# Small score matmuls of two gated recurrences, put into the four column quarters of the matmul array

## The chip, the core and the metric

The kernel runs on one core of a Trainium2 chip. The core has a matmul engine (TensorE, PE in the profile, with its weight loads listed apart as PEld), three engines for elementwise work (VectorE or DVE, ScalarE or ACT, GpSimd or POOL), SyncE (SP) that issues DMAs, an on-chip memory of 128 partitions (SBUF), and the accumulators that TensorE writes (PSUM, 128 partitions, here eight tiles of 512 f32 columns). The metric is the device time of one execution in microseconds (us). The kernel before takes 2109.55 us, the median of three runs (2109.23 to 2110.21).

## The reference

One layer of a decoder trunk in float32: x is 256 rows of 2048. A SwiGLU half-step, a mixer, a second SwiGLU half-step, each with an RMS norm ahead and behind:

```python
h = h + 0.5 * rms_norm(swiglu(rms_norm(h, ffn1_pre), w_gate, w_up, w_down), ffn1_post)
h = h + rms_norm(mixer(rms_norm(h, mix_pre)), mix_post)
h = h + 0.5 * rms_norm(swiglu(rms_norm(h, ffn2_pre), ...), ffn2_post)
```

The mixer multiplies the row block with w_in and runs two linear recurrences, GLA (4 heads, keys of 128, values of 256) and HGRN2 (8 heads, 128 and 128). Both are the same recurrence, with a decay a between 0 and 1 for each key channel:

```python
S_t = diag(a_t) S_{t-1} + k_t v_t^T ;  o_t = S_t^T q_t
# GLA:  q = g_q / sqrt(128), a = sigmoid(code @ w_gk + b) ** (1/16)
# HGRN: q = silu(h_q), k = lc * sigmoid(-h_f), a = lb + lc * sigmoid(h_f)
merged = sigmoid(z_gla + b0) * (o_gla @ w_branch_gla) + sigmoid(z_hgrn + b1) * (o_hgrn @ w_branch_hgrn)
return merged @ w_out
```

## The kernel before, in words

**Matmuls.** The 256 rows are two tiles of 128 (t = 0, 1). Every large matmul is made of three (mm3, lines 145 to 149): the operands are split into a high and a low part in the type fp32r, and high by high, low by high and high by low are added up in PSUM. A weight chunk (two pieces of 128 by 512) is loaded by SyncE into `raw`, ScalarE writes its high part (`whi`, line 141), VectorE the rest (`wlo`, line 143), in a ring of five buffers. Some blocks are multiplied in pairs (gemm_pair, class Blocks): for chosen units of two k pieces (`sevens`) the eight products of a 2 by 2 block product are made from seven, with sums of weights on VectorE and ScalarE (`wsum`, `wsumh`, `wsuml`) and sums of the left operand that are made ahead. `FOUR` names four such units, `SUMS` three. `close` adds the shared sums to an accumulator at the end.

**Attention.** Tokens of a tile of 128 rows attend to earlier ones by levels c = 1, 2, 4, ... 64: at level c, the tile is cut into blocks of 2c tokens, and the queries of a block's right half meet the keys of its left half, each scaled with the decays between them. Behind each level VectorE multiplies kT and qT with the block totals (lines 870 and 873). A token with itself is the diagonal. `attention` (line 827) is a generator: at each `yield` it lets the large matmuls go on. It works on four heads at once, with channels in the partitions (qT, kT, 4 heads by 128 tokens in the columns):
- the diagonal (line 838): four matmuls, one for each head, of all 128 keys by all 128 queries, of which VectorE copies the diagonal into `sc` with a mask (line 840);
- levels under 32 (line 854): four matmuls, one for each head, of all 128 keys by the 64 queries in right halves, of which VectorE copies what lies in a block into `sc` with a mask (line 875);
- levels 32 and 64 (line 861): each block's left keys by its right queries; a block's result stands in the PSUM partitions of its keys, so a level-32 result takes 32 partitions, at 0 or 64. ScalarE copies it into `sc` (line 881);
- `sc` by the values, the state of tile 0 for tile 1, norm, gate, transposition (lines 890 to 934).

These matmuls are in f32, and the trace shows two weight loads and two MATMUL records for each. A matmul whose output stands in 32 of the 128 partitions uses 32 of the array's 128 columns; I call such a part a column quarter.

**What sets the order.** `Side.pump` (line 61) is called between the steps of a large matmul and lets each waiting generator go one step: those in `light` at every pump, the first two in `heavy` (the attentions, in pairs t = 0, 1) at every second one. There are three pairs: GLA, and HGRN for heads 0 to 3 and 4 to 7. On each engine the framework then orders instructions by their place in the program and by when it takes them to be ready, so neighbours on one engine can stand in another order than in the code.

**The end of a half-step.** In `down_proj` (line 567) the last seven k pieces of the second half (`tail`, line 628) are kept, and each accumulator is finished over them in turn; the left operand is split when its first matmul is written (`hkhi` on ScalarE, `hklo` on VectorE). `weigh` takes squares of the accumulator and multiplies it with the post norm's weights.

**The hgrn branch.** `two_gates` multiplies two pairs of gate blocks; behind the second pair stand four blocks of w_branch_hgrn, and `merge` (line 1126) adds each into `ms` on VectorE and transposes it for the last projection.

Of the kernel before, what the change touches and what calls it, by code (L numbers as in the profile page):

```python
# [15 lines left out]
P = 128  # L16
# [63 lines left out]
def kernel(ctx: ExitStack, tc: tile.TileContext, a: dict, out: bass.AP):  # L80
# [154 lines left out]
    class Blocks:  # L235
# [71 lines left out]
        def close(self, t, i):  # L307
            c = self.c[t][i][:, :self.w]
            add(c, c, *self.r[t, i])
# [257 lines left out]
    def down_proj(w_dram, nkt, lhs, sums_of, post, pre, wpost, ys, homes, following):  # L567
# [12 lines left out]
        def weigh(t, n):  # L580
            square(acc[t][n], ss[t], n)
            o = acc[t][n]
            if n < 2:
                o = ys()
            elif pre is None and (t, n) == (NT - 1, 3):

                o = work.tile([P, CB], F32, tag="tmp", name=nm("y"), bufs=3)

            nc.vector.tensor_tensor(o, acc[t][n], wpost[n], op=ALU.mult)
            acc[t][n] = o  # L590

        ahead = []
        for hf in range(2):
# [27 lines left out]
            if not hf:  # L621
                ahead = [split(1, kt) for kt in range(2)]
                for t in range(NT):
                    for i in range(2):
                        b.close(t, i)
                        acc[t][i] = b.c[t][i]
                        weigh(t, i)
        tail = [(kt, split(1, kt, homes[i])) for i, kt in enumerate(range(nkt - DTAIL, nkt))]
        for t in range(NT):
            for n in (2, 3):  # L630
# [6 lines left out]
                b.close(t, n - 2)  # L637
                acc[t][n] = b.c[t][n - 2]
# [119 lines left out]
    def mixer(x, rs, ready, following):  # L758
        xl = lhs_of(x)
        w_in = a["w_in"]  # L760
        with ExitStack() as mctx:
            mp = mctx.enter_context(tc.tile_pool(name="mp", bufs=1, reuse_waits="tile"))
            mp.tile([P, 56], F32, name="mfill")
# [3 lines left out]
            def blk(s, dt=F32):  # L767
                return b2.tile([P, CB], dt, tag="b", name=nm(s), bufs=30)
# [8 lines left out]
            mv = mf[:, :masked * 64].rearrange("p (l c) -> p l c", c=64)  # L777
            nc.scalar.dma_start(mv, a["c_masks"].rearrange("l p c -> p l c"))
# [9 lines left out]
            nc.scalar.dma_start(gk[16:17, :], a["gla_b_gk"])  # L788
            rq = []
# [37 lines left out]
            def attention(t, qT, kT, fT, vs, gates, dv, br, b0):  # L827
# [4 lines left out]
                sc = blk("sc")  # L832
                nc.gpsimd.memset(sc, 0.0)
                yield
                ps = ps_tile()
                for i in range(4):
                    sl = slice(i * P, (i + 1) * P)
                    nc.tensor.matmul(ps[:, sl], lhsT=kT[:, sl], rhs=qT[:, sl], start=True, stop=True)
                nc.vector.tensor_tensor(qT, qT, fT, op=ALU.mult)
                nc.vector.copy_predicated(  # L840
                    tiles4(sc), diag.unsqueeze(1).broadcast_to([P, 4, P]), tiles4(ps))
                yield
                tot, totals, at = fT, blk("tot"), 0
                for lv, c in enumerate(LEVELS):
# [5 lines left out]
                    ps = ps_tile()  # L850
                    if c < 32:
                        for i in range(4):
                            sl = slice(i * P, (i + 1) * P)
                            nc.tensor.matmul(ps[:, i * 64:(i + 1) * 64], lhsT=kT[:, sl],  # L854
                                             rhs=halves(qT[:, sl])[1], start=True, stop=True)
# [18 lines left out]
                    if c < 32:  # L874
                        nc.vector.copy_predicated(
                            halves(sc)[1],
                            masks[:, lv, :, :].rearrange("p h (b c) -> p (h b) c", c=c),
                            ps[:, :CB // 2].rearrange("p (b c) -> p b c", c=c))
                    else:
                        for r0 in range(0, P, 2 * c):  # L880
# [135 lines left out]

            def new_part(i):
# [10 lines left out]
            qT = spawn_T([scaled(q[t], rq[t], "q") for t in range(NT)], "qT")  # L1028
# [12 lines left out]
            diag = mp.tile([P, P], U8, name="diag")  # L1041
            nc.vector.tensor_copy(diag, ident)
            masks = mp.tile([P, masked, 4, 64], U8, name="masks")
# [21 lines left out]
            nc.vector.tensor_tensor(lc, lc, lm, op=ALU.mult)  # L1065

# [173 lines left out]
```

## Time and profile before

| what | value |
|---|---|
| median of the runs | 2109.55 us |
| the profiled execution, its own time | 2109.12 us |
| its span, from first to last instruction | 2107.3 us |
| mean granted TensorE clock | 0.998 |
| HBM read | 404.33 MB, 193 GB/s over the span |
| attentions (lines 838 to 861) | 864 to 1111 us of the span |

A page gives, by engine, the time that it was busy and its instructions; the views of the trace give groups of equal instructions by line, what an engine waited for and who released it, and the instructions in order of time. A group's row reads: line, engine, operation, output and inputs by the program's names, shape, count, then busy time and mean of one, then idle time before it. In a timeline row the first number is the start in us, the second the length, and a bracket gives idle time ahead of it and its releaser. [...]

### The profile page before, as it was taken

What the parts mean: (1) busy time and instruction counts of PE and PEld (TensorE: products, weight loads), DVE (VectorE), ACT (ScalarE), POOL (GpSimd) and SP (SyncE); (2) the same over time, 40 slices, a digit from 0 to 9 for tenths busy, and PEclk for the clock granted to TensorE, in tenths of its full rate; (3) what the DMA queues carried; (4) which work ended last, traced back from release to release, by engine and by line L of the source; (5) the groups of instructions that cost most, each with busy time, mean ns of one, the idle gap of its engine ahead of it and who ended that gap; (6) DMA issues with size and microseconds to landing.
All of it is one profiled execution on the core that took longest, in us unless ns stands there. A gap on an engine that the chain in (4) does not pass through costs nothing.

```text
span 2107.3 us, 27706 instructions
## 1 busy us (share of the span) xinstructions
PE 2094.5 (99%) x9874; PEld 1752.4 (83%) x9874; DVE 1796.9 (85%) x2099; ACT 1194.9 (57%) x1536; POOL 37.7 (2%) x86
## 2 busy tenths in 40 slices
PE   9999999999999999999999999999999999999998
PEld 7888888898888888888888888888888888898886
DVE  7898999999898888756577898578999999999896
ACT  6555565666565575444435555465555556566563
POOL 1000000000000100000000000010000000000000
PEclk9999999999999999999999999999999999999999
DMA  8565756656667556555555666656656666576663
GB/s 268 187 207 189 225 179 206 209 177 219 224 192 237 150 182 194 165 160 142 159 160 169 219 193 210 209 185 186 199 190 201 204 195 213 176 242 191 200 208 131
DMA packets 198012, 408.25 MB, mean 194 GB/s; under 512 B 17185, under 2 KB 25825, under 8 KB 197874
## 3 DMA queue, kind: packets, MB, share of 16 engines
q1 hardware_dynamic: 193168, 399.70, 60.4%
q10 hardware_dynamic: 4706, 6.79, 1.1%
q8 instruction: 77, 1.26, 0.2%
q14 instruction: 61, 0.50, 0.1%
HBM read 404.33 MB, written 2.10 MB: 193 GB/s over the span
## 4 chain that ended last, share of the span: by engine, by line
PE 97%; DVE 1%; DMA 1%; issue 1%; ACT 0%; POOL 0%; SPq 0%; DVEq 0%; POOLq 0%; ACTq 0%
PE c L147 19%; PE c L149 19%; PE c L148 19%; PE mm L147 6%; PE mm L149 6%; PE mm L148 6%; PE p L149 5%; PE p L148 5%; PE p L147 5%; PE ps L377 2%; PE acc L149 1%; PE acc L147 1%; PE acc L148 1%; PE ps L854 1%; DVE h L490 0%
## 5 line engine op out<-in xcount | busy, mean ns | idle before, releaser
L141 ACT ACTIVATE whi<-raw 128x1024 fp32r<-128x1024 f32 (+3 forms) x518 | 539.9, 1048 | 406.2 <-PE mm L148 180.6
L143 DVE TENSOR_TENSOR wlo<-raw,whi 128x1024 fp32r<-128x1024 f32 (+3 forms) x518 | 622.6, 1210 | 146.9 <-ACT whi L141 135.8
L147 PE MATMUL c<-whi,xhi 128*128 128x512 f32 (+1 forms) x1048 | 406.4, 388 | 0.1
L149 PE MATMUL c<-wlo,xhi 128*128 128x512 f32 (+1 forms) x1048 | 403.6, 385 | 0.0
L148 PE MATMUL c<-whi,xlo 128*128 128x512 f32 (+1 forms) x1048 | 403.5, 385 | 0.0
L233 DVE TENSOR_TENSOR wlo<-raw,whi 128x1024 fp32r<-128x1024 f32 (+1 forms) x224 | 261.5, 1202 | 8.9 <-ACT whi L268 5.2
L147 PEld LDWEIGHTS c<-whi,xhi 128*128 128x128 f32 x1048 | 196.8, 188 | 38.2 <-ACT xhi L449 0.5
L149 PEld LDWEIGHTS c<-wlo,xhi 128*128 128x128 f32 x1048 | 196.7, 188 | 38.2 <-DVE wlo L143 0.3
L148 PEld LDWEIGHTS c<-whi,xlo 128*128 128x128 f32 x1048 | 196.9, 188 | 37.0
L233 DVE TENSOR_TENSOR wsuml<-wsum,wsumh 128x1536 fp32r<-128x1536 f32 (+1 forms) x112 | 193.7, 1729 | 36.8 <-ACT wsumh L274 36.6
L148 PE MATMUL c<-whi,hklo 128*128 128x512 f32 x558 | 216.8, 389 | 1.0 <-DVE hklo L143 1.0
L147 PE MATMUL c<-whi,hkhi 128*128 128x512 f32 x558 | 217.0, 389 | 0.0
L149 PE MATMUL c<-wlo,hkhi 128*128 128x512 f32 x558 | 216.8, 388 | 0.0
L272 ACT ACTIVATE whi<-raw 128x1024 fp32r<-128x1024 f32 (+1 forms) x112 | 117.0, 1045 | 170.7 <-DVE raw L233 60.6
L147 PE MATMUL mm<-whi,xhi 128*128 128x512 f32 (+1 forms) x456 | 174.8, 383 | 0.0
L149 PE MATMUL mm<-wlo,xhi 128*128 128x512 f32 (+1 forms) x456 | 171.3, 376 | 0.0
L148 PE MATMUL mm<-whi,xlo 128*128 128x512 f32 (+1 forms) x456 | 171.0, 375 | 0.0
L270 ACT ACTIVATE wsumh<-wsum 128x1024 fp32r<-128x1024 f32 (+1 forms) x112 | 116.7, 1042 | 94.0 <-DVE wsum L233 59.4
L268 ACT ACTIVATE whi<-raw 128x1024 fp32r<-128x1024 f32 (+1 forms) x112 | 116.7, 1042 | 93.4 <-PE c L148 85.4
L233 DVE TENSOR_TENSOR wsum<-raw,raw 128x1024 f32<-128x1024 f32 (+1 forms) x112 | 134.9, 1204 | 19.4 <-DMA raw<-in_ffn_w_down_dram 17.6
L148 PEld LDWEIGHTS c<-whi,hklo 128*128 128x128 f32 x558 | 104.8, 188 | 22.6 <-DVE hklo L143 1.4
L147 PEld LDWEIGHTS c<-whi,hkhi 128*128 128x128 f32 x558 | 104.7, 188 | 21.4
(325 smaller groups left out, 3265.2 us busy)
## 6 DMA issues: line engine op xcount, KB each, us to landing
raw<-in_w_in_dram SPq DMA_DIRECT2D x132, 512.0 KB, 3.9
raw<-in_ffn_w_down_dram SPq DMA_DIRECT2D x124, 512.0 KB, 4.7
raw<-in_ffn_w_up_dram SPq DMA_DIRECT2D x97, 512.0 KB, 4.6
raw<-in_ffn_w_gate_dram SPq DMA_DIRECT2D x96, 512.0 KB, 4.7
raw<-in_ffn_w_gate_dram SPq DMA_DIRECT2D x128, 256.0 KB, 3.7
raw<-in_ffn_w_up_dram SPq DMA_DIRECT2D x126, 256.0 KB, 3.7
raw<-in_ffn_w_down_dram SPq DMA_DIRECT2D x96, 256.0 KB, 3.8
raw<-in_w_in_dram SPq DMA_DIRECT2D x72, 256.0 KB, 3.1
```

Source lines behind the costliest of these rows:

```text
L141: last[0] = nc.scalar.activation(hi, src, AF.Copy)
L143: nc.vector.tensor_tensor(lo, src, hi.bitcast(F32), op=ALU.subtract)
L147: nc.tensor.matmul(ps, lhsT=xhi, rhs=whi, start=start, stop=False)
L148: nc.tensor.matmul(ps, lhsT=xlo, rhs=whi, start=False, stop=False)
L149: nc.tensor.matmul(ps, lhsT=xhi, rhs=wlo, start=False, stop=stop)
L233: return nc.vector.tensor_tensor(o, x, y, op=op)
L268: nc.scalar.activation(ahi, ra, AF.Copy)
L270: nc.scalar.activation(hi[:, 0:2, :], wsum[:, 0:2, :], AF.Copy)
L272: nc.scalar.activation(bhi, rb, AF.Copy)
L377: end = nc.tensor.transpose(dst_ps[:, i * P:(i + 1) * P], src[:, i * P:(i + 1) * P], ident)
L854: nc.tensor.matmul(ps[:, i * 64:(i + 1) * 64], lhsT=kT[:, sl], rhs=halves(qT[:, sl])[1], start=True, stop=True)
```

## The change

Levels under 32 no longer multiply all keys of a head with all its right-half queries: for each head and each 32 tokens, 32 keys meet the 16 queries of right halves among the same 32, and the result goes to PSUM partitions 0, 32, 64 or 96, so that consecutive matmuls use the four column quarters by turns. VectorE's masked copies collect them in `own` (128 by 4 heads by 32), which ScalarE copies into `sc` at level 32. The loops of level 32 are exchanged, so that its two quarters come by turns as well.

The diagonal is taken off TensorE: `dots` multiplies q and k (for HGRN with the row lc, which `lc_row` spreads over all partitions by two matmuls with ones) and adds up over channels on VectorE; ScalarE writes it times an identity into `own`.

```diff
-            def attention(t, qT, kT, fT, vs, gates, dv, br, b0):
-                sc = blk("sc")
-                nc.gpsimd.memset(sc, 0.0)
-                yield
-                ps = ps_tile()
+            def dots(q, k, d, row=None):
+                yield
+                pr = blk("pr")
+                if row is not None:
+                    nc.vector.tensor_tensor(pr, q, row(), op=ALU.mult)
+                    q = pr
+                nc.vector.tensor_tensor(pr, q, k, op=ALU.mult)
+                nc.vector.tensor_reduce(d, tiles4(pr), AX.X, ALU.add)
...
+            def attention(t, qT, kT, fT, d, vs, gates, dv, br, b0):
+                own = mp.tile([P, 4 * 32], F32, tag="own", name=nm("own"), bufs=2)
                 for i in range(4):
-                    sl = slice(i * P, (i + 1) * P)
-                    nc.tensor.matmul(ps[:, sl], lhsT=kT[:, sl], rhs=qT[:, sl], start=True, stop=True)
+                    nc.scalar.activation(own[:, i * 32:(i + 1) * 32], diag, AF.Copy,
+                                         scale=d[:, i:i + 1])
                 nc.vector.tensor_tensor(qT, qT, fT, op=ALU.mult)
-                nc.vector.copy_predicated(
-                    tiles4(sc), diag.unsqueeze(1).broadcast_to([P, 4, P]), tiles4(ps))
...
                     if c < 32:
                         for i in range(4):
-                            sl = slice(i * P, (i + 1) * P)
-                            nc.tensor.matmul(ps[:, i * 64:(i + 1) * 64], lhsT=kT[:, sl],
-                                             rhs=halves(qT[:, sl])[1], start=True, stop=True)
+                            for r0 in range(0, P, 32):
+                                sl = slice(i * P + r0, i * P + r0 + 32)
+                                nc.tensor.matmul(ps[r0:r0 + 32, i * 16:(i + 1) * 16],
+                                                 lhsT=kT[:, sl], rhs=halves(qT[:, sl])[1],
+                                                 start=True, stop=True)
                     else:
-                        for r0 in range(0, P, 2 * c):
-                            for i in range(4):
+                        for i in range(4):
+                            for r0 in range(0, P, 2 * c):
...
+                        if c == 32:
+                            sc = blk("sc")
+                            nc.gpsimd.memset(sc, 0.0)
+                            for r0 in range(0, P, 32):
+                                nc.scalar.copy(
+                                    tiles4(sc)[r0:r0 + 32, :, r0:r0 + 32],
+                                    own[r0:r0 + 32, :].rearrange("p (h c) -> p h c", c=32))
...
+            def lc_row(g):
+                hi, lo = blk("lch", F32R), blk("lcl", F32R)
+                for i in range(4):
+                    sl, w = slice(i * P, (i + 1) * P), lc[:, 4 * g + i:4 * g + i + 1]
+                    nc.scalar.activation(hi[:, sl], ident, AF.Copy, scale=w)
+                    nc.vector.scalar_tensor_tensor(lo[:, sl], ident, w, hi[:, sl].bitcast(F32),
+                                                   op0=ALU.mult, op1=ALU.subtract)
+                yield
+                yield
+                ps = ps_tile()
+                nc.tensor.matmul(ps, lhsT=ones, rhs=hi, start=True, stop=False)
+                nc.tensor.matmul(ps, lhsT=ones, rhs=lo, start=False, stop=True)
+                lc_rows[g] = blk("lcr")
+                nc.scalar.copy(lc_rows[g], ps)
```

For HGRN the key is needed with tokens in the partitions too, so ScalarE makes `hk` from the gate block (one sigmoid of 128 by 512 for each tile and half), and the query block of the second half is multiplied ahead of its gate block. The pool of 128 by 512 buffers has 31 in place of 30.

Three smaller parts of the change lie elsewhere. The left operand of the kept pieces in `down_proj` is split with them; the last of all accumulators is closed into SBUF instead of PSUM; and the last pair of gate blocks uses three seven-product units in place of four:

```diff
-        tail = [(kt, split(1, kt, homes[i])) for i, kt in enumerate(range(nkt - DTAIL, nkt))]
+        tail = []
+        for i, kt in enumerate(range(nkt - DTAIL, nkt)):
+            tail.append((kt, split(1, kt, homes[i])))
+            lhs_h(0, kt)
...
-                b.close(t, n - 2)
-                acc[t][n] = b.c[t][n - 2]
+                acc[t][n] = b.close(t, n - 2, tmp() if at_end(t, n) else None)
...
             def two(sums, c0, c1, ready, *following):
+                four = len(sums) > len(SUMS) and c1 != O_ZH + 3 * CB
                 return gemm_pair([(w_in, c0), (w_in, c1)], CB, xl, sums, ready, following,
-                                 sevens=sorted(sums))
+                                 sevens=FOUR if four else SUMS)
```

How that moves instructions is seen on three places. First TensorE, in the GLA attentions, before: the diagonal of the two tiles (`qT` and `kT` of t = 0 and 1), between matmuls of a large block (`mm`), and 24 matmuls further on level 1.

```order
L149 MATMUL mm_1608_7633<-wlo_7695,xhi_1326_6177 128x512
L838 MATMUL ps_7710<-qT_6423,kT_7130 128x128 x4
L838 MATMUL ps_7717<-qT_6424,kT_7131 128x128 x4
L147 MATMUL mm_1607_7632<-whi_7726,xhi_1311_6082 128x512
L148 MATMUL mm_1607_7632<-whi_7726,xlo_1312_6083 128x512
```

```order
L149 MATMUL mm_1608_7633<-wlo_7745,xhi_1326_6177 128x512
L854 MATMUL ps_7761<-qT_6423,kT_7130 128x64 x4
L854 MATMUL ps_7771<-qT_6424,kT_7131 128x64 x4
L147 MATMUL mm_1607_7632<-whi_7782,xhi_1311_6082 128x512
L148 MATMUL mm_1607_7632<-whi_7782,xlo_1312_6083 128x512
```

The same of the change, at the first of these two places:

```order
L149 MATMUL mm_1614_7664<-wlo_7734,xhi_1326_6177 128x512
L885 MATMUL ps_7750<-qT_6428,kT_7153 32x16 x16
L885 MATMUL ps_7772<-qT_6429,kT_7154 32x16 x16
L147 MATMUL mm_1613_7663<-whi_7795,xhi_1311_6082 128x512
L148 MATMUL mm_1613_7663<-whi_7795,xlo_1312_6083 128x512
```

Level 1 stands where the diagonal stood, with 16 matmuls of 32 by 16 for each tile instead of four of 128 by 64, and each later step of the pair has moved up by one.

Second VectorE, at the end of the first half-step, before: shared sums (`psum`), kept weight pieces (`held`), ring pieces (`wlo`) and the left operand (`hklo`).

```order
L233 TENSOR_TENSOR psum_5875<-psum_5875,p_1129_5297 128x512
L143 TENSOR_TENSOR wlo_5957<-raw_5954,whi_5956 128x1024
L233 TENSOR_TENSOR psum_5875<-psum_5875,p_1131_5299 128x512
L143 TENSOR_TENSOR held_5969<-raw_5966,held_5968 128x1024
L233 TENSOR_TENSOR psum_5876<-psum_5875,p_1130_5298 128x1024
L143 TENSOR_TENSOR held_5975<-raw_5972,held_5974 128x1024
L143 TENSOR_TENSOR wlo_5963<-raw_5960,whi_5962 128x1024
L143 TENSOR_TENSOR held_5981<-raw_5978,held_5980 128x1024
L143 TENSOR_TENSOR hklo_5991<-hT_3785,hkhi_5990 128x512
L143 TENSOR_TENSOR held_5987<-raw_5984,held_5986 128x1024
L143 TENSOR_TENSOR wlo_6000<-raw_5997,whi_5999 128x1024
L143 TENSOR_TENSOR hklo_6007<-hT_3785,hkhi_6006 128x512
```

And of the change, from the same row on:

```order
L233 TENSOR_TENSOR psum_5875<-psum_5875,p_1129_5297 128x512
L143 TENSOR_TENSOR hklo_5955<-hT_3785,hkhi_5954 128x512
L233 TENSOR_TENSOR psum_5875<-psum_5875,p_1131_5299 128x512
L143 TENSOR_TENSOR wlo_5961<-raw_5958,whi_5960 128x1024
L233 TENSOR_TENSOR psum_5876<-psum_5875,p_1130_5298 128x1024
L143 TENSOR_TENSOR hklo_5971<-hT_3785,hkhi_5970 128x512
L143 TENSOR_TENSOR held_5977<-raw_5974,held_5976 128x1024
L143 TENSOR_TENSOR wlo_5967<-raw_5964,whi_5966 128x1024
L143 TENSOR_TENSOR held_5983<-raw_5980,held_5982 128x1024
L143 TENSOR_TENSOR hklo_5987<-hT_4132,hkhi_5986 128x512
L143 TENSOR_TENSOR held_5993<-raw_5990,held_5992 128x1024
L143 TENSOR_TENSOR held_5999<-raw_5996,held_5998 128x1024
```

Three of the four `hklo` now stand ahead of the last two `held`; before, none did, and one stood ahead of the last.

Third VectorE, behind the first pair of the hgrn gates (`sz`), where the last pair begins, before:

```order
L955 SCALAR_TENSOR_TENSOR sz_10844<-c_2172_10488,r_6359,bg_10483 128x512
L233 TENSOR_TENSOR wsum_10899<-raw_10897,raw_10898 128x1024
L233 TENSOR_TENSOR raw_10898<-wsum_10899,raw_10897 128x512
L233 TENSOR_TENSOR wsum_10899<-raw_10898 128x512
L233 TENSOR_TENSOR wlo_10907<-raw_10897,whi_10906 128x1024
L233 TENSOR_TENSOR wlo_10909<-raw_10898,whi_10908 128x1024
L233 TENSOR_TENSOR wsuml_10901<-wsum_10899,wsumh_10900 128x1536
L143 TENSOR_TENSOR wlo_10948<-raw_10945,whi_10947 128x1024
L233 TENSOR_TENSOR wsum_10965<-raw_10963,raw_10964 128x1024
```

And of the change:

```order
L993 SCALAR_TENSOR_TENSOR sz_11296<-c_2190_10940,r_6359,bg_10935 128x512
L143 TENSOR_TENSOR wlo_11352<-raw_11349,whi_11351 128x1024
L233 TENSOR_TENSOR wsum_11369<-raw_11367,raw_11368 128x1024
L233 TENSOR_TENSOR raw_11368<-wsum_11369,raw_11367 128x512
L233 TENSOR_TENSOR wsum_11369<-raw_11368 128x512
L233 TENSOR_TENSOR wlo_11377<-raw_11367,whi_11376 128x1024
```

One unit's sums are gone there; its two chunks stand further on as plain `wlo`.

More of the change, by code (lines that the diff above doesn't have):

```diff
@@ L767, in blk @@
             def blk(s, dt=F32):
[L768 removed]
+                return b2.tile([P, CB], dt, tag="b", name=nm(s), bufs=31)
             def held(w):
@@ L788, in mixer @@
             nc.scalar.dma_start(gk[16:17, :], a["gla_b_gk"])
+            ones = mp.tile([P, P], F32R, name="ones")
+            nc.gpsimd.memset(ones.bitcast(F32), 1.0)
             rq = []
@@ L1039, in mixer @@
             hqT = spawn_T(hqs, "hqT")
-            diag = mp.tile([P, P], U8, name="diag")
-            nc.vector.tensor_copy(diag, ident)
-            masks = mp.tile([P, masked, 4, 64], U8, name="masks")
+            diag = mp.tile([P, 32], F32, name="diag")
+            for r0 in range(0, P, 32):
+                nc.vector.tensor_copy(diag[r0:r0 + 32, :], ident[r0:r0 + 32, r0:r0 + 32])
+            masks = mp.tile([P, masked, 4, 16], U8, name="masks")
             for i in range(4):
@@ L1075, in mixer @@
             for t in range(NT):
[L1076 removed]
+                side.heavy.append(attention(t, qT[t], kT[t], fT[t], dd[t], [vb[0][t], vb[1][t]],
                                             [gb[0][t], gb[1][t]], 256, "g", 0))
             for g in range(2):
[L1081 to L1084 removed]
                 if g == 0:
```

66 lines of the change are left out of this document (45 added, 21 removed).

## The prediction

> **What bounds the kernel now.** I read the page first, then what TensorE waits for, then the groups of the lines that the change touches, and last the timeline around single groups. The page's first part:
>
> ```profile
> PE 2094.5 (99%) x9874; PEld 1752.4 (83%) x9874; DVE 1796.9 (85%) x2099; ACT 1194.9 (57%) x1536; POOL 37.7 (2%) x86
> ```
>
> TensorE is busy for all but 13 us of the span. All that it waited for, longest first:
>
> ```profile
> PE ps L1180 <- POOL idle L1175: 1.3, 1, 1.3
> PE ps L377 <- DVE sz L1129: 1.1, 1, 1.1
> PE c L148 <- DVE hklo L143: 1.0, 1, 1.0
> ```
>
> So time is what TensorE issues, one thing behind the other: a row taken from it shortens the run by its issue time, and a row moved to VectorE or ScalarE is free while they keep up. Busy time of small matmuls overlaps in these records, so I price them by starts, not by durations. How many there are, from the views of lines 854 (levels under 32) and 838 (each key with its own query):
>
> ```profile
> L854 PE MATMUL ps<-hqT,hkT x160: 217/275/275, 977.6 to 1098.2; 128*128 128x64 f32 x160
> L854 PE MATMUL ps<-qT,kT x80: 217/275/275, 871.5 to 903.1; 128*128 128x64 f32 x80
> L838 PE MATMUL ps<-hqT,hkT x32: 270/275/275, 970.3 to 1061.9; 128*128 128x128 f32 x32
> L838 PE MATMUL ps<-qT,kT x16: 270/275/275, 864.2 to 865.9; 128*128 128x128 f32 x16
> ```
>
> A matmul in f32 leaves two records. The 240 are 15 steps of 16 (five levels, three pairs of attentions), the 48 are three steps of 16. TensorE's timeline at one step of each kind, and at one step of level 32:
>
> ```profile
> 977.11 0.39 PE L148 MATMUL mm<-whi,xlo 128*128 128x512 f32 x1
> 977.34 0.39 PE L149 MATMUL mm<-wlo,xhi 128*128 128x512 f32 x1
> 977.56 1.89 PE L854 MATMUL ps<-hqT,hkT 128*128 128x64 f32 x16
> ...
> 979.58 0.39 PE L148 MATMUL mm<-whi,xlo 128*128 128x512 f32 x1
> ```
>
> ```profile
> 970.10 0.39 PE L149 MATMUL mm<-wlo,xhi 128*128 128x512 f32 x1
> 970.32 1.95 PE L838 MATMUL ps<-hqT,hkT 128*128 128x128 f32 x16
> ...
> 972.34 0.40 PE L148 MATMUL mm<-whi,xlo 128*128 128x512 f32 x1
> ```
>
> ```profile
> 1014.56 0.39 PE L149 MATMUL mm<-wlo,xhi 128*128 128x512 f32 x1
> 1014.88 0.90 PE L861 MATMUL ps<-hqT,hkT 128*32 128x32 f32 x32
> ...
> 1016.04 0.39 PE L148 MATMUL mm<-whi,xlo 128*128 128x512 f32 x1
> ```
>
> A 512-column matmul starts 0.23 us behind the last (977.11, 977.34). From the matmul before a step to the second one behind it lie 2.24, 2.24 and 1.48 us; less two normal distances (0.46), a step costs **1.78, 1.78 and 1.02 us**.
>
> **The levels under 32.** A step becomes 32 matmuls, 64 records of 32 keys by 16 queries, which go round the four column quarters. Nothing before has this shape; nearest is level 32, with 32-column records in two quarters, eight in one and then eight in the other. Its records counted by the window in which they have started (the second x is weight loads):
>
> ```profile
> 1014.88:1015.03 0.15, 0.15 (x5) 0.15 (x6) 1.00 0.16 55
> 1014.88:1015.08 0.20, 0.20 (x7) 0.20 (x9) 1.00 0.12 41
> 1014.88:1015.13 0.25, 0.25 (x11) 0.25 (x12) 1.00 0.10 33
> 1014.88:1015.60 0.72, 0.72 (x32) 0.72 (x32) 1.00 0.47 46
> ```
>
> Five start in the first 0.15 us: 0.03 us each while one quarter works alone. Between 1015.08 and 1015.13 four start in 0.05 us, 12.5 ns each: the next quarter had begun while the first still worked through its eight. All 32 take 0.72 us where one queue at 0.03 would take 0.96. So a quarter is a queue of its own at about 0.03 us a record, and two of them run beside each other. What the step costs beyond its records is 1.02 - 0.72 = 0.30 us.
>
> With four quarters by turns each gets 16 of the 64 records: 16 x 0.03 = 0.48 us. Its lower end, 0.48 + 0.30 = 0.78 us a step, needs 7.5 ns from start to start, denser than any row. The upper end of this case takes the densest pace seen: 64 x 12.5 ns + 0.30 = 1.10. I take 0.94, the middle: 0.48, 0.16 for starting four queues and for the second attention's first wait, 0.30. Gain 15 x (1.78 - 0.94) = **-12.6 us**, with ends of -15.0 and -10.2.
>
> [...]
>
> **The diagonal.** Its three steps vanish from TensorE: 3 x 1.78 = **-5.3 us**. VectorE and ScalarE take it over. Added on VectorE: one or two products and a reduction per attention, eight lc differences; removed, beside six diagonal copies, three quarters of the columns of these:
>
> ```profile
> L875 DVE COPY_PREDICATED sc<-masks,ps 128x256 f32<-128x256 uint8 x30 | 16.5, 549 | 0.0
> L881 ACT COPY sc<-ps 32x128 f32<-32x128 f32 x12 | 3.0, 252 | 0.1
> ```
>
> ScalarE gains 24 scalings into own and 24 copies of 32 rows, priced like the second row at 0.25 us: 12 us, and some 6 us of gates and lc rows. Two stretches (us, then TensorE, weight loads, VectorE, ScalarE, GpSimd):
>
> ```profile
> 960.00:1030.00 70.00, 70.00 (x406) 59.49 (x405) 47.09 (x86) 29.86 (x39) 0.00 (x0) 1.00 0.53 149
> 1060.00:1140.00 80.00, 80.00 (x461) 68.03 (x461) 59.60 (x90) 35.88 (x59) 2.58 (x4) 1.00 0.54 158
> ```
>
> ScalarE is idle for 84 of these 150 us and VectorE for 43, so 18 us spread over three pairs hide: 0. Without that cover ScalarE's 18 us would be paid, at most. The memset of sc moves to level 32, where ScalarE's copies wait behind it; queued behind them are weight splits, and the ring holds five chunks.
>
> **Level 32.** Two queues of 16 instead of eight and eight: 0.48 + 0.06 + 0.30 = 0.84 against 1.02, 3 x 0.18 = **-0.5 us**. Level 64 has one column half and is as before.
>
> **What TensorE gets.** Four ones-by-lc matmuls of 512 columns: 4 x 0.23 = **+0.9 us**. In the last pair of gate blocks one seven-product unit becomes eight products, three more matmuls: **+0.7 us**.
>
> **Two stalls.** At the end of ffn1:
>
> ```profile
> 675.77 0.50 PE L148 MATMUL c<-whi,hklo 128*128 128x512 f32 x1 [0.99 <-DVE hklo L143]
> 673.89 1.22 DVE L143 TENSOR_TENSOR wlo<-raw,whi 128x1024 fp32r<-128x1024 f32 x1
> 675.03 1.28 DVE L143 TENSOR_TENSOR hklo<-hT,hkhi 128x512 fp32r<-128x512 f32 x2
> ```
>
> The hklo that TensorE waits for stands behind the last held piece and a wlo. In the new order all three 512-column hklo stand ahead of the last two held. Late next is the last held, some 3 us of TensorE work further on: **-1.0 us**. At the start of the hgrn branch:
>
> ```profile
> 1292.71 1.26 PE L377 MATMUL ps<-ident,sz 128*128 128x128 f32 x8 [1.06 <-DVE sz L1129]
> 1289.63 1.23 DVE L143 TENSOR_TENSOR wlo<-raw,whi 128x1024 fp32r<-128x1024 f32 x1 [1.50 <-PE mm L149]
> 1290.78 1.28 DVE L1128 TENSOR_TENSOR sz<-mm,sz 128x512 f32<-128x512 f32 x2
> 1291.97 1.28 DVE L1129 TENSOR_TENSOR sz<-sz,sz 128x512 f32<-128x512 f32 x2
> ```
>
> The merge stands behind a late weight split. The seven-product unit that goes cost VectorE this shortly before:
>
> ```profile
> 1263.10 1.22 DVE L233 TENSOR_TENSOR wsum<-raw,raw 128x1024 f32<-128x1024 f32 x1
> 1264.35 0.69 DVE L233 TENSOR_TENSOR raw<-wsum,raw 128x512 f32<-128x512 f32 x1
> 1265.08 0.69 DVE L233 TENSOR_TENSOR wsum<-raw 128x512 f32<-128x512 f32 x1
> 1265.69 2.35 DVE L233 TENSOR_TENSOR wlo<-raw,whi 128x1024 fp32r<-128x1024 f32 x2
> 1267.96 1.75 DVE L233 TENSOR_TENSOR wsuml<-wsum,wsumh 128x1536 fp32r<-128x1536 f32 x1
> ```
>
> 6.7 us, of which the two plain chunks keep 2.35: VectorE is 4.3 us less behind, more than the 1.1 us of lateness: **-1.1 us**, with 0 as the other end, since the row order at the merge itself stays. The very last close into SBUF changes a buffer, not a step: 0.
>
> **The sum** against the profiled execution's 2109.12 us (the median of the runs is 2109.55): -12.6 - 5.3 - 0.5 + 0.9 + 0.7 - 1.0 - 1.1 = -18.9, so **2090 us**. Without the levels it is -6.3.
>
> **The rivals.** (1) Starts come one at a time, whatever the quarter: at level 32's mean of 0.72 / 32 = 22.5 ns a step is 1.44 + 0.30 = 1.74 us, the levels give 0.6 instead of 12.6, and the time is 2102. For it: no row shows more than two quarters at work. Against it: the 12.5 ns. (2) The quarters don't overlap at all, and the change doesn't do what it says: 64 x 0.03 + 0.30 = 2.22 us, 15 x 0.44 = +6.6 us, the sum is +0.3, and the time 2109.4: no change. The window counts speak against it. (3) On the slower side: TensorE's instructions can't be supplied as fast as it would take them. Level 32 shows 32 pairs of load and matmul in a burst, a new step has 64. The densest long run of the trace is this (time, TensorE's rows):
>
> ```profile
> 724.00:744.00 20.00, 20.00 (x167) 1.00 0.59 175
> ```
>
> 0.12 us a pair. If the first 32 pairs run by quarters (0.36) and the others arrive at that pace, a step is 0.36 + 3.84 + 0.30 = 4.5 us, 15 x 2.7 = +41 us, and the time is 2144. It decides from the pace at which a step costs 2.20 us, where -6.3 is used up: (2.20 - 0.66) / 32 = 0.048 us a pair. That run was held back by its own columns, so it bounds the supply from one side only. [...] (4) The levels gain, but ScalarE's queue or reused buffers hold weight splits back for 3 to 8 us: 2093 to 2098.
>
> **How the numbers follow.** The forecast 0.55 (2087 to 2093), one start at a time 0.17, a new hold-up 0.14, no overlap 0.06, supply 0.08. Faster by over 0.2% (4.2 us, about what a measurement of this kernel can tell) takes the forecast, (1) and (4): 0.86. Within 0.2%: 0.06; slower: 0.08. The range reaches from 2085 (0.78 a step and quicker records of 16 columns) to 2104 (rival 1 without the second stall's 1.1); outside lie rivals 2 and 3, 0.14, and the edges.
>
> **What would show it.** Right: 15 groups of small matmuls of 32 columns with some 0.6 us from first start to last, the next 512-column matmul 0.9 us later than without them; no step between the transposes and the first level; no wait for hklo at 675. Wrong: these groups take 1.4 us or more (rival 1), starts that thin out in a group's second half (rival 3), or waits of TensorE for whi or wlo between 860 and 1130 us (rival 4).

## The result, and the profile after

| | before | after |
|---|---|---|
| median of the runs | 2109.44 us (4 runs, 2109.23 to 2110.21) | 2087.44 us (4 runs, 2087.23 to 2087.95) |
| profiled execution, its span | 2109.12, 2107.3 us | 2087.65, 2085.7 us |
| mean granted TensorE clock | 0.998 | 0.999 |

The ratio is 0.9895 (95% interval 0.9882 to 0.9909), 22.0 us less; the forecast was 2090, by a sum of -18.9. The engines' busy times of the kernel after, and all that its TensorE waited for:

```profile
PE 2075.6 (100%) x10553; PEld 1730.5 (83%) x10553; DVE 1790.7 (86%) x2116; ACT 1207.8 (58%) x1594; POOL 38.4 (2%) x87
```

```profile
PE ps L1251 <- POOL idle L1246: 1.3, 1, 1.3
PE ps L1255 <- DMA ident<-in_c_ident_dram: 0.2, 1, 0.2
```

The waits for sz and for hklo are gone; what is left belongs to the start. The small matmuls of the levels under 32 (now line 885), then TensorE's timeline at one step of them, and at one step of level 32:

```profile
L885 PE MATMUL ps<-hqT,hkT x640: 176/183/203, 957.4 to 1073.2; 128*32 128x16 f32 x160
L885 PE MATMUL ps<-qT,kT x320: 176/183/203, 863.7 to 891.1; 128*32 128x16 f32 x160
```

```profile
869.46 0.39 PE L148 MATMUL mm<-whi,xlo 128*128 128x512 f32 x1
869.68 0.39 PE L149 MATMUL mm<-wlo,xhi 128*128 128x512 f32 x1
870.00 0.74 PE L885 MATMUL ps<-qT,kT 128*32 128x16 f32 x64
870.67 0.50 PE L147 MATMUL mm<-whi,xhi 128*128 128x512 f32 x1
871.00 0.39 PE L148 MATMUL mm<-whi,xlo 128*128 128x512 f32 x1
...
896.57 0.39 PE L149 MATMUL mm<-wlo,xhi 128*128 128x512 f32 x1
896.89 0.70 PE L892 MATMUL ps<-qT,kT 128*32 128x32 f32 x32
897.51 0.50 PE L147 MATMUL mm<-whi,xhi 128*128 128x512 f32 x1
897.85 0.39 PE L148 MATMUL mm<-whi,xlo 128*128 128x512 f32 x1
```

There are 960 records in 15 groups of 64, as the change says. Priced as in the prediction, from the matmul before the step to the second one behind it less two normal distances, a step costs 871.00 - 869.68 - 0.455 = 0.865 us, against 1.78 before. A step of level 32 costs 897.85 - 896.57 - 0.455 = 0.83. How many of the 64 have started by a time (first x; the window, then TensorE's busy time and count, then the weight loads'):

```profile
869.99:870.05 0.06, 0.05 (x4) 0.05 (x8) 1.00 0.47 171
869.99:870.08 0.09, 0.08 (x8) 0.08 (x12) 1.00 0.40 137
869.99:870.11 0.12, 0.11 (x12) 0.11 (x16) 1.00 0.39 137
869.99:870.14 0.15, 0.14 (x16) 0.14 (x20) 1.00 0.31 109
869.99:870.27 0.28, 0.27 (x32) 0.27 (x34) 1.00 0.21 73
869.99:870.41 0.42, 0.41 (x48) 0.41 (x50) 1.00 0.14 49
869.99:870.56 0.57, 0.56 (x64) 0.56 (x64) 1.00 0.31 50
```

Sixteen start in each 0.14 us, from the first to the last: **8.7 ns a record** on average, with next to no thinning out. The first rows show that they come in rounds of four, one record for each quarter. By their starts in the trace, the second round comes 52 ns behind the first and the next ones 32 ns apart; from about the 36th record on it is 33 ns, after one round of 46.

Not foreseen at all was a gain at the very end. VectorE and ScalarE behind the last matmul, before:

```profile
2099.04 0.60 ACT L432 ACTIVATE sq<-c 128x512 bf16<-128x512 f32 x1 [3.60 <-DVE c L233]
2099.76 0.69 DVE L589 TENSOR_TENSOR y<-c,held 128x512 f32<-128x512 f32 x1 [0.81 <-ACT sq L432]
```

and after:

```profile
2078.00 0.69 DVE L590 TENSOR_TENSOR y<-y,held 128x512 f32<-128x512 f32 x1
2078.06 0.63 ACT L434 ACTIVATE sq<-y 128x512 bf16<-128x512 f32 x1 [3.59 <-DVE y L233]
```

Before, the square and the product read the last accumulator (`c`, in PSUM) one after the other, the product 0.81 us late behind ScalarE. After, both read `y` in SBUF, and run at once.

To find where all 22 us went, I added up, over the whole trace of each kernel, the distance from each 512-column matmul to the next one less the normal 0.227 us, sorted by what stands between them:

| term | predicted | before to after, by starts | change |
|---|---|---|---|
| 15 steps of levels under 32 | -12.6 | 26.85 to 13.21 | -13.6 |
| 3 steps of the diagonal | -5.3 | 5.37 to 0 | -5.4 |
| levels 32 and 64 | -0.5 | 6.90 to 6.44 | -0.5 |
| 512-column matmuls | +0.9, +0.7 | 8384 to 8391, 7 x 0.227 | +1.6 |
| wait at the end of ffn1 | -1.0 | 1.26 to 0 | -1.3 |
| wait at the merge, and a weight split ahead of it | -1.1 | 2.61 to 0.88 | -1.7 |
| from the last matmul's start to the end of the span | 0 | 9.52 to 8.85 | -0.7 |
| the rest | 0 | | -0.1 |

But for rounding they add up to the difference of the spans, -21.6 us.

### The profile page after: what moved, and what is told of

It is laid out like the page before. It is cut to its first block, busy times and chain, and to the rows that moved or that the text cites. A ratio compares the mean times of both kernels' runs of the same rounds, so it can differ in the third digit from the quotient of the medians.

```text
span 2085.7 us, 29137 instructions
## 1 busy us (share of the span) xinstructions
PE 2075.6 (100%) x10553; PEld 1730.5 (83%) x10553; DVE 1790.7 (86%) x2116; ACT 1207.8 (58%) x1594; POOL 38.4 (2%) x87
## 4 chain that ended last, share of the span: by engine, by line
PE 97%; DVE 1%; issue 0%; ACT 0%; DMA 0%; POOL 0%; DVEq 0%; POOLq 0%; ACTq 0%
PE c L147 19%; PE c L149 19%; PE c L148 19%; PE mm L147 6%; PE mm L149 6%; PE mm L148 6%; PE p L148 5%; PE p L149 5%; PE p L147 5%; PE ps L379 2%; PE acc L149 1%; PE acc L147 1%; PE acc L148 1%; DVE h L492 0%; PE ps L885 0%
## 5 line engine op out<-in xcount | busy, mean ns | idle before, releaser
L149 PEld LDWEIGHTS c<-wlo,hkhi 128*128 128x128 f32 x558 | 104.8, 188 | 21.6
```

Of the source, the lines that this page charges most:

```text
L149: nc.tensor.matmul(ps, lhsT=xhi, rhs=wlo, start=False, stop=stop)
```

## The experiments

Two theories of the main term stood against each other. In the prediction's, each column quarter is a queue of its own and only the turns keep four of them busy. The rival is that smaller matmuls are simply shorter, or that one limit holds the whole array. The other runs take single parts of the change back.

**blocks: no turns.**

```diff
-                        for i in range(4):
-                            for r0 in range(0, P, 32):
+                        for r0 in range(0, P, 32):
+                            for i in range(4):
```

> The changed kernel with the two loops of the levels under 32 exchanged: the same matmuls, but all four heads of one column quarter (eight records) before the next quarter. Theory A (each quarter is a queue of its own, about 0.035 us a record, and only turns keep four of them busy): the records come at the pace at which level 32 ran in blocks of eight before, 22.5 ns, so a step costs 64 x 22.5 ns + 0.31 = 1.75 us instead of 0.87, 15 x 0.88 = +13 us, 2100.7; without any overlap 64 x 0.035 + 0.31 = 2.55 us and 2112.7. Theory B (a record of 16 columns is simply short, the order is nothing): 2087.4.

Measured: 2098.72 us, 11.3 more than the changed kernel; ratio to before 0.995 (0.9935 to 0.9965). A step in TensorE's timeline, and its records by window:

```profile
877.28 0.39 PE L149 MATMUL mm<-wlo,xhi 128*128 128x512 f32 x1
877.60 1.50 PE L885 MATMUL ps<-qT,kT 128*32 128x16 f32 x64
879.03 0.50 PE L147 MATMUL mm<-whi,xhi 128*128 128x512 f32 x1
```

```profile
877.59:877.75 0.16, 0.15 (x5) 0.15 (x5) 1.00 0.00 0
877.59:878.79 1.20, 1.19 (x59) 1.19 (x60) 1.00 0.61 72
877.59:878.92 1.33, 1.32 (x64) 1.32 (x64) 1.00 0.57 72
```

1.32 us for 64 records is 21 ns each on average, and the same sum by starts is 1.63 us a step. This average is not the pace of one quarter. While the first quarter works alone, five records of 16 columns start in 0.15 us, as many as of 32 columns at level 32 before, and the last five, when only the last quarter is left, start 32 ns apart too. In between two quarters overlap. The trace doesn't name a record's quarter, but all 64 starts fit, within 1 ns, eight series of eight (four quarters, two attentions): the second record 53 ns behind the first, the others 31.7 ns apart, and each series 153 ns behind the one before, when that has three records left to start. The 32 starts of level 32 before fit four such series as well.

So one quarter took a record in 32 ns, at 16 columns here as at 32 before. Of the 0.91 us that a step gained, 0.75 needs the turns; the other 0.16 is left in blocks because neighbouring quarters overlap there too. With no overlap at all a step would take 64 x 0.032 + 0.31 = 2.36 us by this pace (an estimate), more than the 1.78 before the change. The rival that order is nothing falls.

**pairs: two quarters by turns.**

```diff
-                        for i in range(4):
-                            for r0 in range(0, P, 32):
+                        for i, r0 in [(i, r + s) for r in (0, 64) for i in range(4) for s in (0, 32)]:
```

> The changed kernel with the levels under 32 going round two quarters by turns (first 0 and 32, then 64 and 96) instead of four. Theory A: two queues at 0.035 us a record give 17 ns from start to start, 64 x 17.3 ns + 0.31 = 1.42 us a step, 15 x 0.55 = +8.3 us, 2095.7. Theory B (order is nothing): 2087.4. Theory C (what limits is one start per 8.7 ns for the whole array, and two quarters are enough to reach it): 2087.4 too, with records still 8.7 ns apart.

Measured: 2090.61 us, 3.2 more than the changed kernel; ratio 0.9911 (0.9895 to 0.9928). The records by window:

```profile
870.65:870.79 0.14, 0.13 (x8) 0.13 (x10) 1.00 0.21 73
870.65:870.95 0.30, 0.29 (x24) 0.29 (x26) 1.00 0.10 34
870.65:871.40 0.75, 0.74 (x64) 0.74 (x64) 1.00 0.40 49
```

64 records in 0.74 us are 11.6 ns each on average, where theory A had 17.3 and theory C 8.7. The first eight start in 0.14 us, 16 ns apart in the mean: that is theory A's pace, two quarters of 32 ns each. The next sixteen start in 0.16 us, 10 ns apart, because the second pair of quarters begins 160 ns behind the first, while the first still has three records a quarter to go. So theory A had the pace right, and its sum left out that one pair overlaps the next; theory C falls.

**twice: the same matmuls issued a second time.**

```diff
-                        for i in range(4):
+                        for i in (0, 1, 2, 3, 0, 1, 2, 3):
```

> The changed kernel with each of the small matmuls of levels under 32 issued a second time behind the first round, into the same place: 128 records a step instead of 64. Theory A: 64 more records at 8.7 ns are 0.55 us a step, 15 x 0.55 = +8.3 us, 2095.7, and the step's fixed part of 0.31 us stays. Rival (the supply of instructions): the second half thins out; at 0.12 us a pair of load and matmul it would be 32 x 0.12 x 15 = +58 us, 2145.

Measured: 2096.24 us, 8.8 more; ratio 0.9939 (0.9924 to 0.9954). By window:

```profile
870.11:870.67 0.56, 0.55 (x64) 0.55 (x67) 1.00 0.17 18
870.11:871.24 1.13, 1.12 (x128) 1.12 (x128) 1.00 0.44 54
```

The second 64 come as fast as the first, so a run of 128 records is supplied as well as one of 64. The step grows by 0.56 us, and 0.31 us of it is fixed.

**wide: all 32 queries instead of 16.**

```diff
-                                nc.tensor.matmul(ps[r0:r0 + 32, i * 16:(i + 1) * 16],
-                                                 lhsT=kT[:, sl], rhs=halves(qT[:, sl])[1],
+                                nc.tensor.matmul(ps[r0:r0 + 32, i * 32:(i + 1) * 32],
+                                                 lhsT=kT[:, sl], rhs=qT[:, sl],
                                                  start=True, stop=True)
...
-                            ps[:, :64].rearrange("p (b c) -> p b c", c=c))
+                            halves(ps[:, :P])[1])
```

> The changed kernel with all 32 queries of each 32 tokens instead of the 16 in right halves: the same 64 records a step, four quarters by turns, 32 columns each. One quarter alone takes a record each 19 ns at 16 columns and 31.6 ns at 32. Theory A (the array as a whole takes a load and a matmul per 8.7 ns, which four quarters at 32 columns, 31.6 / 4 = 7.9 ns, still reach): no change, 2087.4, a step 0.87 us. Theory B (each quarter is the limit, at 35 ns when four are busy, and more columns lengthen that by 12 ns): 47 / 4 = 11.8 ns a record, a step 1.06 us, 15 x 0.19 = +2.9 us, 2090.3.

Measured: 2088.18 us, 0.7 more; ratio 0.9898 (0.9882 to 0.9915). By window:

```profile
870.39:870.53 0.14, 0.13 (x15) 0.13 (x18) 1.00 0.10 29
870.39:870.97 0.58, 0.57 (x64) 0.57 (x64) 1.00 0.26 42
```

Twice the columns cost 0.01 us a step here (0.57 against 0.56), and 0.03 with the matmul that follows. So theory B falls. That the array as a whole is the limit, as theory A has it, does not follow: both theories took 19 ns for one quarter alone at 16 columns, which is the mean of the overlapping quarters in blocks. With 32 ns for one quarter at either width, four quarters come to 8 ns a record at 16 columns and at 32, and the first half of a step shows that in both (fifteen started in 0.13 us here, sixteen in 0.14 at 16 columns). A limit of each quarter is enough for all these runs, and none of them needs one of the whole array. Which part of the chip sets the 32 ns, and why a round takes 33 ns later in a step, is not shown. Of the 0.7 us, 0.4 by starts is a short wait for hklo at the end of ffn1 (677 us), which the changed kernel just misses.

**level64: level 64 in quarters.**

```diff
-                                nc.tensor.matmul(ps[r0:r0 + c, i * c:(i + 1) * c],
-                                                 lhsT=kT[:, k0:k0 + c],
-                                                 rhs=qT[:, k0 + c:k0 + 2 * c],
-                                                 start=True, stop=True)
+                                for s in range(0, c, 32):
+                                    nc.tensor.matmul(ps[r0 + s:r0 + s + 32, i * c:(i + 1) * c],
+                                                     lhsT=kT[:, k0 + s:k0 + s + 32],
+                                                     rhs=qT[:, k0 + c:k0 + 2 * c],
+                                                     start=True, stop=True)
```

(Line 892; level 32 is unchanged by it.)

> The changed kernel with level 64 in column quarters as well: each matmul of 64 keys becomes two of 32 keys in two quarters by turns, 32 records of 64 columns a step instead of 16. Theory A (a record of one quarter is bound by the quarter, 0.035 us as at 16 columns): 16 records a quarter, 0.56 us instead of 0.93, 3 x 0.37 = -1.1 us, 2086.3. Rival (64 columns must stream, 0.05 to 0.06 us a record in each quarter): 16 x 0.058 = 0.93, no change, 2087.4.

Measured: 2087.73 us, no difference; ratio 0.99 (0.9885 to 0.9915). The step of the changed kernel, and of this one:

```profile
903.18 1.15 PE L892 MATMUL ps<-qT,kT 128*64 128x64 f32 x16
```

```profile
903.81 1.09 PE L893 MATMUL ps<-qT,kT 128*32 128x64 f32 x32
```

The rival holds. A half of 64 columns by 64 queries took a record each 58 ns (16 in the changed kernel, by starts); cut in two, each of the two quarters took one each 55 ns, with the same 64 columns in each. A step was 0.06 us shorter by that.

**diag_pe: the diagonal on TensorE again.**

```diff
-                for i in range(4):
-                    nc.scalar.activation(own[:, i * 32:(i + 1) * 32], diag, AF.Copy,
-                                         scale=d[:, i:i + 1])
+                nc.gpsimd.memset(own, 0.0)
+                yield
+                ps = ps_tile()
+                for i in range(4):
+                    sl = slice(i * P, (i + 1) * P)
+                    nc.tensor.matmul(ps[:, sl], lhsT=kT[:, sl], rhs=qT[:, sl], start=True, stop=True)
                 nc.vector.tensor_tensor(qT, qT, fT, op=ALU.mult)
+                for r0 in range(0, P, 32):
+                    nc.vector.copy_predicated(
+                        own[r0:r0 + 32, :].rearrange("p (h c) -> p h c", c=32),
+                        diag[r0:r0 + 32, :].unsqueeze(1).broadcast_to([32, 4, 32]),
+                        tiles4(ps)[r0:r0 + 32, :, r0:r0 + 32])
```

(`dots`, `lc_row` and the sigmoids into `hk` go with their tiles.)

> The changed kernel with the diagonal on TensorE again (a step of four 128 by 128 matmuls for each attention, copied into own with a mask), and without the products, the reductions, the lc rows and the extra sigmoids. Theory A (the move gains the three steps, 5.4 us, and pays four matmuls, 0.9 us; the work on VectorE and ScalarE is hidden): +4.5 us, 2091.9. Rival (part of what was moved is paid on TensorE as waits): less than that, and 2087.4 if it is all paid.

Measured: 2097.26 us, 9.8 more, twice what was expected; ratio 0.9943 (0.9928 to 0.9958). The three steps were there at 1.79 us each, and no new wait. The excess lay in 512-column matmuls of the mixer, some of which came 231 to 235 ns after the last instead of 227. A group of them, here and in the changed kernel:

```profile
L148 PE MATMUL mm<-whi,oT 128*128 128x512 f32 x128 | 50.5, 395 | 0.0
L149 PE MATMUL mm<-wlo,oT 128*128 128x512 f32 x128 | 50.5, 395 | 0.0
```

```profile
L149 PE MATMUL mm<-wlo,oT 128*128 128x512 f32 x128 | 49.9, 390 | 0.0
L148 PE MATMUL mm<-whi,oT 128*128 128x512 f32 x128 | 49.8, 389 | 0.0
```

oT lives in the pool of 31 buffers, and the tiles that I had taken out stand ahead of that pool: every buffer had moved by 288 bytes. Three runs test that, each by the size of the filler tile `mfill` (120 columns in the changed kernel, 56 before).

**diag_pe2, shifted, filler56.** The first is diag_pe with the filler at 192 columns, the second the changed kernel with 112, the third with 56:

```diff
-            mp.tile([P, 120], F32, name="mfill")
+            mp.tile([P, 112], F32, name="mfill")
```

> The kernel with the diagonal on TensorE again, and its filler tile 288 bytes larger, so that every buffer of the attention stands where it stands in the changed kernel (the tiles that went had moved all of them by 288 bytes). Theory A (the 5 us too much of the run before came from where the buffers stand, and the diagonal itself is worth 5.4 - 0.9 us): 2087.4 + 4.5 = 2091.9, and the matmuls of whi by oT take 389 to 390 ns again instead of 395. Rival (the masked copies or the lost work on VectorE delay TensorE a little everywhere): 2097 as before.

> The changed kernel with nothing but its filler tile 32 bytes smaller, so that the 31 buffers start at 96 instead of 0 modulo 128 bytes, as they did in the first run with the diagonal on TensorE. Theory A (where the buffers stand sets how long the 512-column matmuls that read them take): +4 to +5 us, 2092, with whi by oT at 395 ns. Rival (no effect of the place): 2087.4.

> The changed kernel with its filler tile at 56 columns as before the change: the 31 buffers move by 256 bytes and still start at a multiple of 128 bytes from where they stood. Theory A (what costs is a start off the multiples of 128, as the run with 32 bytes less showed): no change, 2087.4, whi by oT at 389 ns, so this edit is worth nothing by itself. Rival (the place modulo 512 counts, and the edit kept it): +2 to +5 us, 2090 to 2092.

Measured: 2092.82 us for diag_pe2 (0.9921, 0.9906 to 0.9936), 2092.51 for shifted (0.9919, 0.9904 to 0.9934), 2087.61 for filler56 (0.9897, 0.9881 to 0.9914). The group of whi by oT in shifted:

```profile
L148 PE MATMUL mm<-whi,oT 128*128 128x512 f32 x128 | 50.6, 395 | 0.0
L149 PE MATMUL mm<-wlo,oT 128*128 128x512 f32 x128 | 50.5, 395 | 0.0
```

With nothing but 32 bytes less of filler the changed kernel loses 5.1 us, 4.6 of them by starts in plain 512-column matmuls. So theory A holds for all three, and the change's own edit of the filler, 256 bytes, is worth nothing by itself. With the buffers back in place the diagonal costs 5.4 us. By starts it is 4.35 us up to the last matmul, for the 4.5 expected; the other 1.1 lies between VectorE's last row and the end of the span (4.3 us against 3.2), was there in diag_pe too, and stays unexplained. That 4.35 comes so near to 4.5 is in part chance: the first matmul with weights (line 147) starts at 6.78 us in this trace and at 7.48 in that of the changed kernel, which takes 0.7 off, and a short wait for hklo at 677 us adds 0.4.

**four_back, lhs_late, close_psum.** Each takes one of the smaller parts back:

```diff
-                four = len(sums) > len(SUMS) and c1 != O_ZH + 3 * CB
+                four = len(sums) > len(SUMS)
```

> The changed kernel with four seven-product units again in the last pair of gate blocks. Theory A (that unit's sums make VectorE late for the merge in the hgrn branch): three matmuls fewer, -0.7 us, and the wait for sz comes back with what follows it, +1.1 to +1.6 us: +0.4 to +0.9 us, 2087.8 to 2088.3. Rival (the wait went for another reason, such as the new order of VectorE's work): no wait for sz, -0.7 us, 2086.7.

```diff
-            lhs_h(0, kt)
```

> The changed kernel with the left operand of the kept pieces split again when its first matmul is written. Theory A: TensorE waits for hklo once more at the end of the first half-step, +1.0 to +1.3 us, 2088.4 to 2088.7. Rival (the wait depends on how the weights happened to land): 2087.4.

```diff
-                acc[t][n] = b.close(t, n - 2, tmp() if at_end(t, n) else None)
+                acc[t][n] = b.close(t, n - 2)
```

> The changed kernel with the very last accumulator closed into PSUM again. The prediction's step (a buffer changes, no step): 2087.4. Rival (the closing sum and the product behind it on VectorE are shorter with an operand in SBUF, and the end of the run waits for them): +0.5 us, 2087.9.

Measured: 2088.91 us (0.9906, 0.9891 to 0.992), 2088.61 (0.9904, 0.9887 to 0.992) and 2088.49 (0.9905, 0.989 to 0.992), so 1.5, 1.2 and 1.1 more. These are near what a time can tell, so the rows decide. TensorE at the merge in four_back, at the end of ffn1 in lhs_late, and VectorE's last product in close_psum:

```profile
1271.38 0.39 PE L147 MATMUL mm<-whi,oT 128*128 128x512 f32 x1
1273.25 1.26 PE L379 MATMUL ps<-ident,sz 128*128 128x128 f32 x8 [1.48 <-DVE sz L1200]
...
1274.58 0.39 PE L149 MATMUL mm<-wlo,oT 128*128 128x512 f32 x1
```

```profile
675.58 0.50 PE L148 MATMUL c<-whi,hklo 128*128 128x512 f32 x1 [0.71 <-DVE hklo L143]
```

```profile
2080.68 0.69 DVE L590 TENSOR_TENSOR y<-c,held 128x512 f32<-128x512 f32 x1 [0.81 <-ACT sq L434]
```

All three waits are back. In four_back the step at the merge costs 1274.58 - 1271.38 - 0.455 = 2.75 us instead of 0.88, and 0.3 us is lost at a late weight split before it; less three matmuls (0.7) that is the 1.5 measured. The cause was as theory A had it, its price higher. In lhs_late theory A holds, and by starts another 0.5 us is lost at the same place of the second half-step (2058 to 2061 us), where the kernel before had no wait. In close_psum the product stands behind the square as before the change: 0.5 us from the last matmul to the end, which is the rival's number. The rest of its 1.1 is no work of this edit that the trace shows: its runs spread from 2087.95 to 2090.19, and in the longest, which is the profiled one, TensorE waited 1.4 us for the first load of `ident` instead of 0.2.

## Why the prediction was right, and where not

- **The levels under 32** (-12.6 predicted, -13.6 by starts). The step came out at 0.865 us instead of 0.94 (two of the fifteen, where the second attention came late, took 0.93 and 1.03). The mechanism was right: a quarter is a queue of its own at about 0.03 us a record (32 ns, with one quarter at work in blocks, two in pairs, four in the changed kernel), and without the turns 0.75 us of a step's gain is gone (blocks). What was mis-sized is the 0.16 us added to 16 x 0.03 for starting four queues and for the second attention's first wait. The 64 records took 0.55 us from the first start to the last, which is 16 x 0.032 = 0.51 and 0.04 more; the second attention's wait came in two steps of fifteen, at 0.06 and 0.17 us. That 32 columns could stand in for 16 was taken without a test before the run, and held: the pace at 16 columns was no quicker, so the low end of the range, which reckoned with quicker records, was out of reach by this term.
- **Rival 1**, one start at a time at 22.5 ns, falls by the 8.7 ns, and rival 2 with it: four quarters in turn start four records in 32 ns. Rival 3, the supply, falls by twice: 128 loads and 128 matmuls came at 0.0087 us a pair, where it would have decided from 0.048. The 0.12 us of the prediction's long run are those of its 264-column matmuls; by starts, those of 384 columns stood 0.173 us apart in the same trace, those of 512 0.227.
- **The diagonal** (-5.3, by starts -5.4) and the four lc matmuls: diag_pe2 gives +4.35 up to the last matmul, where 5.4 - 0.9 = 4.5 was expected, with the chance in it that is named above. The work on VectorE and ScalarE is hidden, as said. The two stretches of the prediction in the kernel after (us, TensorE, weight loads, VectorE, ScalarE, GpSimd):

```profile
960.00:1030.00 70.00, 70.00 (x618) 57.52 (x617) 46.27 (x81) 38.27 (x75) 4.52 (x8) 1.00 0.56 159
1060.00:1140.00 80.00, 80.00 (x595) 66.15 (x595) 60.40 (x85) 42.87 (x73) 2.86 (x4) 1.00 0.58 175
```

  ScalarE is busy 15 us longer in them than before (81.1 against 65.7) and VectorE as long as before, though the kernel after is some 10 to 20 us further on in its work. TensorE has no wait there, so rival 4 did not come.
- **Level 32**: 0.83 us a step for the 0.84 predicted. Its two quarters took 0.032 us a record each.
- **The two stalls** went for the reasons given, and both were sized too small. At the end of ffn1 the price was the wait of 0.99 us alone; by starts it was 1.378 + 0.335 - 0.455 = 1.26, since the matmul behind the wait started 1.378 us after the one ahead of it, and the next one 0.335 us after that. At the merge the range had 0 as its other end; the lateness of VectorE was the cause (four_back), and it also held a weight split before the merge, 1.7 us in all.
- **The last close** at 0 was the term that failed outright: "changes a buffer, not a step". With the buffer in SBUF ScalarE and VectorE read at once (0.06 us apart), and that gave 0.5 us (close_psum). With the accumulator in PSUM the product waited 0.81 us, before and in close_psum, with it in SBUF not at all. What put the wait there, the trace does not say.
- **Not priced at all** was the filler. It cost nothing as the change set it (filler56), and 32 bytes less of it cost 5.1 us (shifted).

## What to carry to other kernels

Matmuls with few output partitions should go round the column quarters by turns: here the order of two loops was worth 11 us of 2099. Count how many records each quarter has to take before making tiles smaller: here one quarter took a record each 32 ns at 16 columns as at 32, so 16 columns instead of 32 bought 0.01 us of a step's 0.57, and cutting the 64-column matmuls of level 64 in two gave 2087.73 us against 2087.44. An average distance over a burst need not be the pace of one quarter: in blocks neighbouring quarters overlapped, and the average was 21 ns; the first and the last starts, where one worked alone, showed its 32. And when a tile is added or taken away ahead of a pool that TensorE reads, look at where the pool then starts, before blaming or praising the edit itself: here 32 bytes cost 5.1 us.

## What was not expected of the hardware

The distance of f32 records (two for each matmul) by quarters at work and columns, from the runs above and the rows of before:

| quarters at work | 16 columns | 32 columns | 64 columns |
|---|---|---|---|
| one | 32 ns (blocks, first and last five) | 32 ns (before, first five) | |
| two | 16 ns (pairs, first eight) | 16 ns (0.50 us for 32, after) | 28 ns (0.87 us for 32, level64) |
| four | 8 ns in the first half of a step, 8.7 over all (after) | 8 ns in the first half, 8.9 over all (wide) | |

Two quarters halved the distance and four halved it again, at 16 columns and at 32: each quarter kept its 32 ns (33 later in a step) with one, two or four at work. At 64 columns a quarter took 55 ns. Quarters overlapped also when one followed the other (blocks): eight records of a quarter held the next one up by 153 ns, not by the 0.24 us or more from their first start to their last.

With the pool of buffers 32 bytes lower than in the changed kernel (shifted), 512-column matmuls that read it were longer by 4 to 8 ns in the groups of oT and xs (such as whi by oT 395 ns instead of 389, whi by xs 397 instead of 389), and the kernel by 5.1 us; a move by 256 bytes made no difference (filler56, 2087.61 us against 2087.44). Moves by other amounts than 32, 256 and 288 bytes were not tried, so it is not shown that multiples of 128 bytes are what counts, as the theory for filler56 has it.
